# Attention heads in pairs: transposes, scores and value products of two heads in one run each, at fixed places; the gating of the attention branch behind the casts of gate a; the gate logits turned by full-size transposes; the upper halves first in the first query projection

## The chip, the cores and the metric

The kernel runs on one core of a Trainium2 chip. The metric is the time of one execution of the program on the device, in microseconds. The times of before are from three runs; the profile is of one more execution of its own.

## What is computed

An encoder trunk of two layers over 256 tokens of width 1024, all in float32. Each layer normalises its input, multiplies it by one wide matrix `w_in` (11 segments), and feeds two branches: a gated DeltaNet in both directions (with a short convolution over q, k and v) and differential attention. Gates close both branches, two projections and a sigmoid gate each merge them, and an output projection is added to the input. The attention branch is what the change touches:

```python
proj = h @ w_in[l]        # q_a, k_a, v_a, ab_a, z_a, q_b, k_b, v_b, z_b, gate_a, gate_b
# differential attention: 8 heads, each with two maps of width 64 and values of width 128
s = einsum('nbhqd,nbhkd->nbhqk', q_blk, k); p = softmax(s)
a = p[0] - lam * p[1]
o = einsum('bhqk,bhkd->bhqd', a, v)
o = rmsnorm(o, subln_w) * (1.0 - lambda_init);  y_b = o * silu(z_b)
merged = sigmoid(gate_a) * (y_a @ w_pa[l]) + sigmoid(gate_b) * (y_b @ w_pb[l])
```

`ab_a` holds the logits of DeltaNet's decay and write strength, 32 per token.

## The kernel before, in words

**Projections.** The 256 tokens are two tiles `m` of 128. To keep float32 accuracy, every weight is split into an upper half `hi` (rounded) and a lower half `lo = raw - hi`, and so is the activation; three products are added up: activation's upper part with hi (L324), with lo (L325), and its lower part with hi (L326). Weights come in four pairs of k-tiles (`kp`): one DMA of 512 KB into `raw`, a cast on ScalarE (L308, `hi_...`), a subtraction on VectorE (L310, `lo_...`). hi and lo have two buffers each, so the cast of a pair can begin when TensorE has used the pair two before. A name such as lo_zb012 is layer 0, half 1 of segment zb, pair 2; pp_zb010 is its sum for m = 0. `proj_tm` runs one such projection of 512 columns: 8 k-tiles by 2 m by 3 products, 48 matmuls.

**PSUM.** Eight banks: four in rotation for projections' sums (`banks2`, two at a time), two (`banks2_c`, `bank_c`) and two more (`bank`). The convolution's sums (pf_q, pf_k, pf_v), the scores of heads 0 and 1 and the sums of zb1 share the rotation of four; zb0's sums and the scores of the later heads use the pair `banks2_c`.

**Order.** Each engine works through its own queue in order. The tile scheduler sets the queues from the program text, priorities and explicit edges: `behind(x)` places an instruction after x. `mark` keeps instructions to be named so, and `place(n)` is the last matmul of k-tile n, counted on from zb0's first through zb0, zb1, za0, za1, gb0 and on, eight a projection.

**Attention.** The projections follow one another: qk (queries and keys, rotated by L602 to L605, turned by L608 and brought to `qkT` by ScalarE), conv v in between, zb0, zb1, za0, za1 (z of both branches), gb0, gb1 and ga0, ga1 (gates). Between their matmuls lie, head by head:
- `scores`: four 64-row matmuls (L1067; in the profile two records each, eight to a head), both maps side by side in the two halves of the array's rows, each map into a bank of its own (sc..1, sc..0); then VectorE's maxima (`mx`, L1075, one per map), ScalarE's exponentials with sums (L1077, four), and on VectorE a reciprocal (L1080), the factor `cc` (L1081) and two steps that subtract the second map (L1083, `es`);
- `turn`: four transposes of the map (L1094, `at`), copied by ScalarE (L1096, `aT`);
- `attend`: four products with v (L1105, `av`), copied by ScalarE into `ob` (L1109) and squared there with sums (L1111) for the norm.

Head h - 1 is turned shortly before the scores of head h, its product follows them. Heads 0 and 1 are scored within and right behind zb0.

VectorE has more to do there: the convolution of v (L679, `cvv`, four steps a channel tile, reading pf_v011 in PSUM until the last of them; L690), block transposes (L135), SiLU of z (L399, after ScalarE's tanh L398) and a forward substitution for DeltaNet's triangular solve (L868 and L869, `fstmp` and `X`), whose 31 steps are paced by the casts.

**Gating.** When the squares of all heads are there, `rb` is made (L1242 to L1245, with a power on POOL), and `gate_yb(i)` multiplies ob, rb and the gate (L1197) and turns the result in blocks (L249). Half 0 is placed behind casts of gb1, half 1 behind those of ga0.

**Logits.** `abp` (L630) has the 64 rows of both halves of the logits' weights, copied to `abT`; two matmuls with `id2` (L636, in the profile 64 rows by 32 columns) add the halves and turn them.

## Time and profile before

| | before |
|---|---|
| median of 3 runs | 742.87 us (742.01 to 742.99) |
| profiled execution | 742.73 us |
| its span, first to last instruction | 740.8 us |
| mean granted TensorE clock | 0.997 |
| busy: PE, DVE, ACT, POOL | 99%, 79%, 65%, 19% |
| moved from and to HBM | 182 GB/s over the span |

Times in rows of the profile are in us from the span's start. PE is TensorE's matmuls, PEld its weight loads, DVE VectorE, ACT ScalarE, POOL GpSimd. A row of a timeline gives start, duration (of a group: to the end of the last), engine, line, operation, output and inputs, shapes, and how many in a row; idle time and what ended it stand in brackets. A matmul's duration is longer than the distance to the next one, since matmuls are pipelined, so the distance between starts is what counts.

### The profile page before, as it was taken

To read this page: it belongs to the slowest core of one execution; us is meant where nothing else is said; L and a number is where in the kernel's file an instruction comes from. 1 tells how busy PE (TensorE), PEld (TensorE's weight loads), DVE (VectorE), ACT (ScalarE), POOL (GpSimd) and SP (SyncE) were. 2 spreads that over 40 slices of the span, in tenths; PEclk is the share of its full clock that TensorE was granted. 3 is DMA by queue.
4 is the path that set the end of the run, shared out by engine and by line. 5 is a ranking of instruction groups with operands and counts; after the bars stand their busy time and mean duration, and the time that the engine had idled before them with its cause. 6 is when DMAs were issued, how large, how long until landed. Compare 5 with 4: busy or idle time off the path is not lost.

```text
span 740.8 us, 13649 instructions
## 1 busy us (share of the span) xinstructions
PE 732.1 (99%) x5034; PEld 635.6 (86%) x5034; DVE 588.5 (79%) x1119; ACT 479.5 (65%) x1018; POOL 140.9 (19%) x223
## 2 busy tenths in 40 slices
PE   9999999999999999999999999999999999999996
PEld 6999889987888899888889899889788888998885
DVE  8696898999986885578667769999999769728782
ACT  6666875667876586645456578555787748665552
POOL 6004110112022433100000150202110514311000
PEclk9999999999999999999999999999999999999998
DMA  8755667776766473567674466767766736436641
GB/s 264 239 173 171 172 181 195 209 207 203 208 181 163 136 208 104 173 205 246 201 234 138 129 192 184 212 175 236 200 173 197 203 116 196 150 124 204 213 142 57
DMA packets 73732, 135.43 MB, mean 183 GB/s; under 512 B 12912, under 2 KB 13921, under 8 KB 73666
## 3 DMA queue, kind: packets, MB, share of 16 engines
q1 hardware_dynamic: 64750, 113.65, 51.6%
q0 software_dynamic: 7936, 19.35, 9.1%
q10 hardware_dynamic: 980, 1.58, 0.6%
q8 instruction: 39, 0.64, 0.4%
q14 instruction: 27, 0.22, 0.1%
HBM read 125.53 MB, written 9.01 MB: 182 GB/s over the span
## 4 chain that ended last, share of the span: by engine, by line
PE 96%; ACT 2%; issue 1%; DVE 1%; POOLq 0%; POOL 0%; DVEq 0%; ACTq 0%
PE pp_vb L369 4%; PE pp_qk L325 4%; PE pp_qk L326 3%; PE pp_qk L324 3%; PE sc L1067 2%; PE pp_o L369 2%; PE pp_za L325 2%; PE pf_k L385 2%; PE pf_v L385 2%; PE pf_v L389 2%; PE pp_ga L324 2%; PE pp_gb L324 2%; PE pp_zb L324 2%; PE pf_q L387 2%; PE pf_k L389 2%; PE pf_k L387 2%
## 5 line engine op out<-in xcount | busy, mean ns | idle before, releaser
L325 PE MATMUL pp_qk<-lo_qk,hT 128*128 128x512 f32 x128 | 50.5, 394 | 0.3
L326 PE MATMUL pp_qk<-hi_qk,hT 128*128 128x512 f32 x128 | 49.9, 390 | 0.0
L310 DVE TENSOR_TENSOR lo_qk<-raw_qk,hi_qk 128x1024 fp32r<-128x1024 f32 x32 | 39.1, 1221 | 12.0 <-ACT hi_qk L308 11.7
L324 PE MATMUL pp_qk<-hi_qk,hT 128*128 128x512 f32 x128 | 45.1, 393 | 0.0
L308 ACT CAST hi_qk<-raw_qk 128x1024 fp32r<-128x1024 f32 x28 | 29.4, 1049 | 23.4 <-PE pp_qk L326 12.7
L1077 ACT ACTIVATE es<-sc,mx 128x256 f32<-128x256 f32 x64 | 29.6, 473 | 19.5 <-DVE mx L1075 19.5
L385 PE MATMUL pf_q<-hT,hi_q 128*128 128x256 f32 x128 | 36.1, 285 | 0.0
L387 PE MATMUL pf_q<-hT,hi_q 128*128 128x256 f32 x128 | 35.9, 284 | 0.0
L385 PE MATMUL pf_k<-hT,hi_k 128*128 128x256 f32 x128 | 35.9, 286 | 0.0
L387 PE MATMUL pf_k<-hT,hi_k 128*128 128x256 f32 x128 | 35.9, 285 | 0.0
L385 PE MATMUL pf_v<-hT,hi_v 128*128 128x256 f32 x128 | 35.8, 285 | 0.0
L387 PE MATMUL pf_v<-hT,hi_v 128*128 128x256 f32 x128 | 35.8, 284 | 0.0
L389 PE MATMUL pf_q<-hT,lo_q 128*128 128x256 f32 x128 | 35.2, 288 | 0.0
L310 DVE TENSOR_TENSOR lo_pb<-raw_pb,hi_pb 128x1024 fp32r<-128x1024 f32 x16 | 19.6, 1225 | 18.9 <-ACT hi_pb L308 18.9
L389 PE MATMUL pf_v<-hT,lo_v 128*128 128x256 f32 x128 | 34.6, 288 | 0.0
L389 PE MATMUL pf_k<-hT,lo_k 128*128 128x256 f32 x128 | 34.3, 284 | 0.0
L308 ACT CAST hi_pa<-raw_pa 128x1024 fp32r<-128x1024 f32 x16 | 16.9, 1055 | 22.2 <-PE pp_pa L326 16.1
L679 DVE SCALAR_TENSOR_TENSOR cvq<-pf_q,cw,cvq 128x254 f32<-128x254 f32 (+1 forms) x64 | 30.0, 479 | 0.9 <-ACT cvq L675 0.4
L679 DVE SCALAR_TENSOR_TENSOR cvv<-pf_v,cw,cvv 128x254 f32<-128x254 f32 (+1 forms) x64 | 29.9, 479 | 0.1
L325 PEld LDWEIGHTS pp_qk<-lo_qk,hT 128*128 128x128 f32 x128 | 24.0, 188 | 6.6 <-DVE lo_qk L310 1.6
L679 DVE SCALAR_TENSOR_TENSOR cvk<-pf_k,cw,cvk 128x254 f32<-128x254 f32 (+1 forms) x64 | 28.5, 476 | 1.5 <-ACT cvk L675 0.9
L310 DVE TENSOR_TENSOR lo_pa<-raw_pa,hi_pa 128x1024 fp32r<-128x1024 f32 x16 | 19.6, 1224 | 11.2 <-ACT hi_pa L308 11.2
(416 smaller groups left out, 2535.1 us busy)
## 6 DMA issues: line engine op xcount, KB each, us to landing
raw_qk<-in_w_in_dram SPq DMA_DIRECT2D x32, 512.0 KB, 3.8
raw_k<-in_w_in_dram SPq DMA_DIRECT2D x16, 512.0 KB, 4.6
raw_q<-in_w_in_dram SPq DMA_DIRECT2D x16, 512.0 KB, 3.7
raw_v<-in_w_in_dram SPq DMA_DIRECT2D x16, 512.0 KB, 3.8
raw_zb<-in_w_in_dram SPq DMA_DIRECT2D x16, 512.0 KB, 4.0
raw_za<-in_w_in_dram SPq DMA_DIRECT2D x16, 512.0 KB, 3.8
raw_ga<-in_w_in_dram SPq DMA_DIRECT2D x16, 512.0 KB, 4.6
raw_pb<-in_w_pb_dram SPq DMA_DIRECT2D x16, 512.0 KB, 4.0
```

Source lines behind the costliest of these rows:

```text
L308: high = (V.tensor_copy if kp in turned else S.copy)(hi[:, :, :n], raw[:, :, :n]).ins
L310: mark[nm, kp] = high, V.tensor_tensor(lo[:, :, :n], raw[:, :, :n], hi[:, :, :n].bitcast(F32), ALU.subtract).ins
L324: T.matmul(o, act[kt // 4][:, 0, kt % 4, ts_], hi, start=kt == 0, stop=False)
L325: T.matmul(o, act[kt // 4][:, 0, kt % 4, ts_], lo, start=False, stop=False)
L326: mark["proj"] = T.matmul(o, act[kt // 4][:, 1, kt % 4, ts_], hi, start=False, stop=kt == KT - 1).ins
L369: mark["proj"] = T.matmul(o, act[kt // 4][:, pa, kt % 4, ts_], ws[kt][1 + pw], start=kt == 0 and n_ == 0, stop=kt == KT - 1 and n_ == 2).ins
L385: T.matmul(o, hi[:, cs], act[kt // 4][:, 0, kt % 4, :], start=first, stop=False, skip_group_check=True)
L387: T.matmul(o, hi[:, cs], act[kt // 4][:, 1, kt % 4, :], start=False, stop=False, skip_group_check=True)
L389: T.matmul(o, lo[:, cs], act[kt // 4][:, 0, kt % 4, :], start=False, stop=done, skip_group_check=True)
L679: V.scalar_tensor_tensor(ca[:, o0:o1], acc[:, b, o0 + sft : o1 + sft], cw[:, j, cb : cb + 1], ca[:, o0:o1], ALU.mult, ALU.add)
L1067: mm = T.matmul(sp[n][:, qt * SEQ : (qt + 1) * SEQ], qkT[h // 4][rows, 0, h % 4, qt * P : (qt + 1) * P], qkT[h // 4][rows, 1, h % 4, :], s ...
L1077: S.activation(es[:, n, qt, :], spv[:, qt, :], AF.Exp, bias=mx[:, n, qt : qt + 1], accum_out=s_all[:, h, n, qt : qt + 1])
```

## The change

It has four parts.

1. **Heads in pairs.** For p = 0 to 3 both heads of the pair before are turned (places 7, 12, 20, 27 of the count of k-tiles; heads 6 and 7 at 35), then both heads of pair p are scored, the second right behind the first, then the value products of the pair before go in one run into one bank and are copied at once. Head 2 and all even ones now take banks of the rotation of four; odd ones keep the pair.
2. **Gating behind casts.** `gate_yb` takes one tile (i, m) at a time: tile (0, 0) behind the cast of gb1's pair 2, the other three behind ga0's pairs 0, 1 and 2.
3. **Logits by full tiles.** `abT` gets 128 rows (64 of them zeros set by POOL) and is turned by two full transposes; the halves are added on VectorE.
4. **Upper first.** In the first query projection (qk00) all products with hi of the first two k-tiles come first, then those with lo.

```diff
@@ -109,8 +109,6 @@
     G.memset(ident, 1.0)
     G.affine_select(out=ident, in_=ident, compare_op=ALU.is_equal, fill=0.0,
                     base=0, pattern=[[1, P]], channel_multiplier=-1)
-    id2 = const.tile([64, 32], F32, name="id2")
-    V.tensor_tensor(id2, ident[0:64, 0:32], ident[0:64, 32:64], ALU.add)
     G.memset(tri, 1.0)
     for d, sg in ((0, 1), (1, -1)):
         G.affine_select(out=tri[:, d, :], in_=tri[:, d, :], compare_op=ALU.is_ge,
@@ -313,11 +311,20 @@
                 yield 2 * kp + k, hi[:, k, :n], lo[:, k, :n]
 
     def proj_tm(act, w, c0, n, evac, nm, places=(None,) * 4, spare=(), later=None, turned=(), between=None,
-                banks=None, held=None, first=(), raws={}):
+                banks=None, held=None, first=(), raws={}, upper=0):
 
         accs = (banks or banks2)(f"pp_{nm}")
-        for kt, hi, lo in weights(w, c0, n, nm, places, later=later, spare=spare, turned=turned, held=held,
-                                  first=first, raws=raws):
+        parts = weights(w, c0, n, nm, places, later=later, spare=spare, turned=turned, held=held,
+                        first=first, raws=raws)
+        ws = [next(parts) for _ in range(upper)]
+        for part in range(2 if ws else 0):
+            for kt, hi, lo in ws:
+                for m in range(NM):
+                    for pa in range(2 - part):
+                        mark["proj"] = mark["done", nm, kt] = T.matmul(
+                            accs[m][:, :n], act[kt // 4][:, pa, kt % 4, m * P : (m + 1) * P], lo if part else hi,
+                            start=not (kt or pa or part), stop=False).ins
+        for kt, hi, lo in parts:
             for m in range(NM):
                 ts_ = slice(m * P, (m + 1) * P)
                 o = accs[m][:, :n]
@@ -610,7 +617,7 @@
                     mark["qkT", m] = S.mul(qkT[i][:, s_, :, m * P : (m + 1) * P],
                                            pt.rearrange("p (b t) -> p b t", b=4), (DH ** -0.5, 1.0)[s_]).ins
                 proj_tm(hT, wl, (C_QB, C_KB)[s_] + 512 * i, 512, evac_qk, f"qk{l}{s_}{i}",
-                        turned=(0, 1) if (s_, i) == (0, 1) else ())
+                        turned=(0, 1) if (s_, i) == (0, 1) else (), upper=2 if (s_, i) == (0, 0) else 0)
 
 
 
@@ -629,13 +636,14 @@
             for part in range(2):
                 T.matmul(abp[0:64, :SEQ], wabr[:, kt, :], hT[kt // 4][:, part, kt % 4, :],
                          start=kt == 0 and part == 0, stop=kt == KT - 1 and part == 1)
-        abT = work.tile([64, SEQ], F32, tag="w2c", name=f"abT{l}", bufs=3)
-        mark["ab"] = S.copy(abT, abp[0:64, :SEQ]).ins
-        abq = bank_c(f"abq{l}")
+        abT = work.tile([P, SEQ], F32, tag="w2c", name=f"abT{l}", bufs=3)
+        G.memset(abT[64:P], 0.0)
+        mark["ab"] = S.copy(abT[0:64], abp[0:64, :SEQ]).ins
+        abq = bank_c(f"abq{l}")[:, :SEQ].rearrange("p (m c) -> p m c", m=NM)
         for m in range(NM):
-            T.matmul(abq[:, m * 32 : (m + 1) * 32], abT[:, m * P : (m + 1) * P], id2,
-                     start=True, stop=True)
-        V.tensor_copy(ab.rearrange("p m c -> p (m c)"), abq[:, :64])
+            T.transpose(abq[:, m, :], abT[:, m * P : (m + 1) * P], ident)
+        V.tensor_copy(ab, abq[:, :, 0:32])
+        V.tensor_tensor(ab, ab, abq[:, :, 32:64], ALU.add)
 
         a_ = small.tile([P, NM, 32], F32, tag="ga_", name=f"ga_{l}")
         V.tensor_scalar(a_[:, :, 0:16], ab[:, :, 0:16], -1.0, None, ALU.mult)
@@ -1059,7 +1067,7 @@
         def scores(h, after):
             es = work.tile([P, 2, NM, SEQ], F32, tag="w4a", name=f"es{l}{h}", bufs=2)
             mx = small.tile([P, 2, NM], F32, tag="mx", name=f"mx{l}{h}")
-            sp = (banks2 if h < 2 else banks2_c)(f"sc{l}{h}")
+            sp = (banks2_c if h > 1 and h % 2 else banks2)(f"sc{l}{h}")
             for qt in range(NM):
                 for n in (1, 0):
                     rows = slice(64 * n, 64 * n + 64)
@@ -1096,19 +1104,21 @@
                 S.copy(aT.rearrange("p k q -> p (k q)"), ap_)
             return aT
 
-        def attend(h, aT, after):
+        def attend(h0, maps, after):
             with tc.high_priority(offset=HP):
-                op_ = bank(f"av{l}{h}")
+                op_ = bank(f"av{l}{h0}").rearrange("p (q h e) -> p q h e", q=NM, h=2)
+                for h, aT in enumerate(maps, h0):
+                    for qt in range(NM):
+                        for kt in range(NM):
+                            with behind(after):
+                                T.matmul(op_[:, qt, h - h0], aT[:, kt, qt * P : (qt + 1) * P],
+                                         vb[h // 4][:, kt, h % 4 * P : h % 4 * P + P],
+                                         start=kt == 0, stop=kt == NM - 1)
+            oh = ob[h0 // 4][:, :, h0 % 4 * P : h0 % 4 * P + 2 * P].rearrange("p q (h e) -> p q h e", h=2)
+            S.copy(oh, op_)
+            for h in range(2):
                 for qt in range(NM):
-                    for kt in range(NM):
-                        with behind(after):
-                            T.matmul(op_[:, qt * P : (qt + 1) * P], aT[:, kt, qt * P : (qt + 1) * P],
-                                     vb[h // 4][:, kt, h % 4 * P : h % 4 * P + P],
-                                     start=kt == 0, stop=kt == NM - 1)
-            oh = ob[h // 4][:, :, h % 4 * P : h % 4 * P + P]
-            S.copy(oh, op_[:, :SEQ].rearrange("p (q e) -> p q e", q=NM))
-            for qt in range(NM):
-                S.activation(sqj[:, :P], oh[:, qt, :], AF.Square, accum_out=ssb[:, qt, h : h + 1])
+                    S.activation(sqj[:, :P], oh[:, qt, h], AF.Square, accum_out=ssb[:, qt, h0 + h : h0 + h + 1])
 
         zb = e4(f"zb{l}", "ex")
         za = [work.tile([P, NM, 512], F32, tag="w4c", name=f"za{l}_{i}", bufs=4) for i in range(2)]
@@ -1165,16 +1175,12 @@
         es = {}
         for p in range(4):
             z_part((zb, za)[p // 2], (C_ZB, C_ZA)[p // 2], ("zb", "za")[p // 2], p % 2)
-            for h in (2 * p, 2 * p + 1):
-                at = place((3, 7, 11, 15, 19, 23, 27, 31)[h])
-                aT = turn(h - 1, es[h - 1], at) if h > 2 else None
-                es[h] = scores(h, mark["at", h - 1] if h > 2 else place((3, 7, 12)[h]))
-                if h > 2:
-                    attend(h - 1, aT, mark["sc", h])
-                elif h == 1:
-                    attend(0, turn(0, es[0], place(7)), place(7))
-                elif h:
-                    attend(1, turn(1, es[1], place(11)), place(13))
+            two, at = (2 * p, 2 * p + 1), place((7, 12, 20, 27)[p])
+            maps = [turn(h, es[h], at) for h in range(two[0] - 2, two[0]) if p]
+            for h in two:
+                es[h] = scores(h, mark["sc", h - 1] if h % 2 else mark["at", h - 1] if p else at)
+            if p:
+                attend(two[0] - 2, maps, mark["sc", two[1]])
             substitute(names[p])
             if p == 0:
                 place_v(mark[f"zb{l}0", 1][0])
@@ -1227,9 +1233,9 @@
         wgb = big.tile([P, 2, 2, 512], F32R, tag="p8", name=f"wgb{l}", bufs=4)
         def last_head():
             weigh_q(0, 0, place(32))
-            aT = turn(7, es[7], place(34))
+            maps = [turn(h, es[h], place(35)) for h in (6, 7)]
             weigh_q(0, 1, place(36))
-            attend(7, aT, place(39))
+            attend(6, maps, place(38))
             weigh_q(1, 0, place(39))
 
         gtb = gate(C_GB, f"gb{l}", "ev",
@@ -1245,15 +1251,17 @@
         V.scalar_tensor_tensor(rb, rb, 0.5 * (1.0 - lam0), r0, ALU.mult, ALU.mult)
 
         ybT, yb_sent = pair(f"ybT{l}"), {}
-        def gate_yb(i):
-            at = [mark[f"ga{l}0", 1 + m][1] if i else mark[f"gb{l}1", 2 + m][1] for m in range(NM)]
+        def gate_yb(i, m, at):
             gated(lambda i, m: heads4(ob[i][:, m, :]), zb, rb, nw[:, 1:2], ybT, f"yb{l}",
-                  after={(i, m): at[m] for m in range(NM)}, halves_=(i,), sent=yb_sent)
-            for m in range(NM):
-                fetch(*yb_sent[i, m], None)
-
-        gate_yb(0)
-        gta = gate(C_GA, f"ga{l}", "eo", (lambda: gate_yb(1), None))
+                  (m,), {(i, m): at}, (i,), yb_sent)
+            fetch(*yb_sent[i, m], None)
+
+        def gate_others():
+            for kp, (i, m) in enumerate(((0, 1), (1, 0), (1, 1))):
+                gate_yb(i, m, mark[f"ga{l}0", kp][1])
+
+        gate_yb(0, 0, mark[f"gb{l}1", 2][1])
+        gta = gate(C_GA, f"ga{l}", "eo", (gate_others, None))
         for i, m in ((0, 0), (0, 1), (1, 0), (1, 1)):
             split_B(ybT[i], yb_sent[i, m][0], m, nw[:, 1:2], mark[f"ga{l}{i}", 2 + m])
         branch(ybT, w_pb[l], gtb, f"pb{l}")
```

Lines below the edit in `proj_tm` move: the products are L331 to L333 there, the casts L306 and L308, the scores L1075, mx L1083, the exponentials L1085.

**TensorE at zb0's end** (pp_zb00 is zb0's sum, pp_zb01 zb1's; sc00 and sc01 are the scores of heads 0 and 1). Before:

```order
L324 MATMUL pp_zb001_2026<-hi_zb003_2081,hT0_1_127 128x512
L325 MATMUL pp_zb001_2026<-lo_zb003_2082,hT0_1_127 128x512
L326 MATMUL pp_zb001_2026<-hi_zb003_2081,hT0_1_127 128x512
L1067 MATMUL sc011_2125<-qkT0_0_313 128x256
L1067 MATMUL sc010_2124<-qkT0_0_313 128x256
L1067 MATMUL sc011_2125<-qkT0_0_313 128x256
L1067 MATMUL sc010_2124<-qkT0_0_313 128x256
L324 MATMUL pp_zb010_2168<-hi_zb010_2170,hT0_0_126 128x512
L325 MATMUL pp_zb010_2168<-lo_zb010_2171,hT0_0_126 128x512
```

After:

```order
L332 MATMUL pp_zb001_2026<-lo_zb003_2082,hT0_1_125 128x512
L333 MATMUL pp_zb001_2026<-hi_zb003_2081,hT0_1_125 128x512
L1075 MATMUL sc001_2106<-qkT0_0_311 128x256
L1075 MATMUL sc000_2105<-qkT0_0_311 128x256
L1075 MATMUL sc001_2106<-qkT0_0_311 128x256
L1075 MATMUL sc000_2105<-qkT0_0_311 128x256
L1075 MATMUL sc011_2125<-qkT0_0_311 128x256
L1075 MATMUL sc010_2124<-qkT0_0_311 128x256
L1075 MATMUL sc011_2125<-qkT0_0_311 128x256
L1075 MATMUL sc010_2124<-qkT0_0_311 128x256
L331 MATMUL pp_zb010_2153<-hi_zb010_2155,hT0_0_124 128x512
L332 MATMUL pp_zb010_2153<-lo_zb010_2156,hT0_0_124 128x512
```

Head 0's four score matmuls, which stood amid zb0 between pairs 1 and 2, now stand at its end ahead of head 1's four; zb1's first matmul follows both.

**VectorE between lo_zb011 and lo_zb012** (mx00 and mx01 are the maxima of heads 0 and 1, thv the tanh of the convolution). Before:

```order
L310 TENSOR_TENSOR lo_zb011_2189<-raw_zb011_2190,hi_zb011_2188 128x1024
L1075 TENSOR_REDUCE mx01_2123<-sc011_2125 128x2
L399 SCALAR_TENSOR_TENSOR zb0_0_385<-zb0_0_385,pp_zb001_2026 128x512
L1075 TENSOR_REDUCE mx01_2123<-sc010_2124 128x2
L869 TENSOR_TENSOR X0_377<-X0_377,fstmp0_378 128x15x17
L690 SCALAR_TENSOR_TENSOR thv012_1890<-thv012_1890,cvv013_1893 128x256
L310 TENSOR_TENSOR lo_zb012_2207<-raw_zb012_2208,hi_zb012_2206 128x1024
```

After, the first twelve rows:

```order
L308 TENSOR_TENSOR lo_zb011_2174<-raw_zb011_2175,hi_zb011_2173 128x1024
L1083 TENSOR_REDUCE mx00_2104<-sc001_2106 128x2
L687 SCALAR_TENSOR_TENSOR cvv013_1893<-pf_v011_1738,cw0_298,cvv013_1893 128x254
L406 SCALAR_TENSOR_TENSOR zb0_0_385<-zb0_0_385,pp_zb001_2026 128x512
L1083 TENSOR_REDUCE mx00_2104<-sc000_2105 128x2
L877 TENSOR_TENSOR X0_377<-X0_377,fstmp0_378 128x15x17
L1088 RECIPROCAL cc00_2117<-s_all0_381 128x2
L698 SCALAR_TENSOR_TENSOR thv012_1890<-thv012_1890,cvv013_1893 128x256
L1083 TENSOR_REDUCE mx01_2123<-sc011_2125 128x2
L876 TENSOR_TENSOR fstmp0_378<-la0_375,X0_377 128x256
L1083 TENSOR_REDUCE mx01_2123<-sc010_2124 128x2
L133 STREAM_TRANSPOSE tb_v012_1901<-thv012_1890 128x512
```

Before, five steps stood between the two casts. After, the maxima of both heads stand there, and behind the rows shown come two factors cc, one more reciprocal, the four es steps of both heads and five steps of the substitution; only then comes lo_zb012, and lo_zb013 right behind it.

**VectorE from lo_ga000 to lo_ga002** (ktm are DeltaNet's keys, ob the attention's outputs). Before:

```order
L310 TENSOR_TENSOR lo_ga000_2896<-raw_ga000_2897,hi_ga000_2895 128x1024
L1004 TENSOR_TENSOR ktm0_360<-ktm0_360,kds0_372 128x512 x2
L310 TENSOR_TENSOR lo_ga001_2914<-raw_ga001_2915,hi_ga001_2913 128x1024
L1004 TENSOR_TENSOR ktm0_360<-ktm0_360,kds0_372 128x512 x2
L1197 SCALAR_TENSOR_TENSOR ob0_1_384<-ob0_1_384,rb0_2862,zb0_1_386 128x128 x4
L249 STREAM_TRANSPOSE zb0_1_386<-ob0_1_384 128x4x4x32
L310 TENSOR_TENSOR lo_ga002_2932<-raw_ga002_2933,hi_ga002_2931 128x1024
```

After:

```order
L308 TENSOR_TENSOR lo_ga000_2877<-raw_ga000_2878,hi_ga000_2876 128x1024
L1012 TENSOR_TENSOR ktm0_360<-ktm0_360,kds0_372 128x512 x2
L1203 SCALAR_TENSOR_TENSOR ob0_0_383<-ob0_0_383,rb0_2854,zb0_0_385 128x128 x4
L308 TENSOR_TENSOR lo_ga001_2895<-raw_ga001_2896,hi_ga001_2894 128x1024
L1012 TENSOR_TENSOR ktm0_360<-ktm0_360,kds0_372 128x512 x2
L1203 SCALAR_TENSOR_TENSOR ob0_1_384<-ob0_1_384,rb0_2854,zb0_1_386 128x128 x4
L247 STREAM_TRANSPOSE zb0_0_385<-ob0_0_383 128x4x4x32
L247 STREAM_TRANSPOSE zb0_1_386<-ob0_1_384 128x4x4x32
L308 TENSOR_TENSOR lo_ga002_2913<-raw_ga002_2914,hi_ga002_2912 128x1024
```

Four more products with rb and one more block transpose now stand ahead of lo_ga002; they stood ahead of lo_ga000 before. Ahead of these rows lo_gb013 and one step of B have moved behind rb.

## Prediction

> **What bounds the kernel now.** I read the page first: busy time, clock and chain.
>
> ```profile
> PE 732.1 (99%) x5034; PEld 635.6 (86%) x5034; DVE 588.5 (79%) x1119; ACT 479.5 (65%) x1018; POOL 140.9 (19%) x223
> ...
> PEclk9999999999999999999999999999999999999998
> ...
> PE 96%; ACT 2%; issue 1%; DVE 1%; POOLq 0%; POOL 0%; DVEq 0%; ACTq 0%
> ```
>
> TensorE is busy throughout at full clock, and 96% of the chain that ended last is its own work. A matmul taken away there is time gained; any new wait of TensorE is time lost. So the second reading is TensorE's waits: only one is long, and it lies before the first real matmul.
>
> ```profile
> PE idle L410 <- DVE ones L407: 1.1, 1, 1.1
> ```
>
> The third is who could make it wait. The change moves work in the stretch where head 0 and head 1 start, so I asked for the busy time of that window. The columns are the length, then busy time (and count) of PE, PEld, DVE, ACT and POOL, the clock, the DMA share and GB/s.
>
> ```profile
> 155.00:185.00 30.00, 30.00 (x151) 23.53 (x149) 29.97 (x68) 22.56 (x57) 4.12 (x8) 1.00 0.68 198
> ```
>
> This is the row that decides. The page's 79% for VectorE is an average; in these 30 us it has 0.03 us free. Whatever holds VectorE up here goes through its casts (lo_zb) to TensorE.
>
> **What the change saves on TensorE.** First the scores. The timeline of the second run of head scores, with two looks inside it:
>
> ```profile
> 170.84 0.40 PE L325 MATMUL pp_zb<-lo_zb,hT 128*128 128x512 f32 x1
> 171.07 0.40 PE L326 MATMUL pp_zb<-hi_zb,hT 128*128 128x512 f32 x1
> 171.40 1.14 PE L1067 MATMUL sc<-qkT 64*128 64x256 f32 x8
> 172.46 0.50 PE L324 MATMUL pp_zb<-hi_zb,hT 128*128 128x512 f32 x1
> 172.80 0.40 PE L325 MATMUL pp_zb<-lo_zb,hT 128*128 128x512 f32 x1
> ...
> 171.72 0.81 PE L1067 MATMUL sc<-qkT 64*128 64x256 f32 x6
> 171.94 0.60 PE L1067 MATMUL sc<-qkT 64*128 64x256 f32 x4
> ```
>
> Matmuls of 512 columns follow each other every 0.23 us (170.84, 171.07), and pairs of score records, one in each half of the rows, every 0.22 (171.72, 171.94). From 171.07 to 172.80 pass 1.73 us; two 512s (0.46) and four pairs (0.86) explain 1.32. Going into the run of 64-row matmuls and out again costs the other 0.41. Two heads in one run leave 8 runs of 16: four times 0.41, so 1.64 us a layer.
>
> The Trainium skill's page "TensorEngine Tiling (Array Packing)", under Key Properties, says that changing the tiling mode drains TensorE, without a figure. The drain of 128 cycles at 2.4 GHz that "TensorE: Matmul & The Clock Gate" gives (step-by-step, 4) would be an estimated 0.05 us each way, and with that the eight runs would bring 0.8 us in all instead of 3.3; the measured 0.41 a run decides.
>
> The small projection abq and the first products of queries are the other two savings:
>
> ```profile
> 27.17 0.28 PE L389 MATMUL pf_k<-hT,lo_k 128*128 128x256 f32 x1
> 27.38 0.63 PE L636 MATMUL abq<-id,abT 64*128 64x32 f32 x4
> 27.94 0.39 PE L385 MATMUL pf_k<-hT,hi_k 128*128 128x256 f32 x1
> 28.16 0.28 PE L387 MATMUL pf_k<-hT,hi_k 128*128 128x256 f32 x1
> ...
> 164.84 0.66 PE L608 MATMUL qkt<-ident,stg 128*128 128x128 f32 x4
> ...
> 80.20 0.61 PE L324 MATMUL pp_qk<-hi_qk,hT 128*128 128x512 f32 x2
> 80.96 0.50 PE L325 MATMUL pp_qk<-lo_qk,hT 128*128 128x512 f32 x1
> ...
> 79.68 1.22 DVE L310 TENSOR_TENSOR lo_qk<-raw_qk,hi_qk 128x1024 fp32r<-128x1024 f32 x1
> ```
>
> 27.17 to 28.16 is 0.99, of which two 256s would be 0.24: abq costs 0.75. Four full-width transposes end 0.66 after their start, so I take 0.11 each and 0.22 for the new two: 0.53 saved. At 80.96 a lo matmul starts 0.30 later than 80.20 + 2 x 0.23 and with 0.1 of restart behind it: it waited for the cast that ended at 80.90. That is the third pair of k-tiles of qk00; with upper first the first pair's hi buffer is free four matmuls sooner, and the order puts that lo ahead of the convolution steps. I take the 0.41 as gone. The memset on POOL, one more add of 64 columns and half as many copies of ob are hidden by engines that are idle there (POOL 19%); uncovered, each is below 1 us.
>
> Saved: 1.64 + 0.53 + 0.41 = 2.6 us a layer, 5.2 in all.
>
> **What it adds: waits at four places in each layer.** Their prices come from these rows of VectorE's and ScalarE's timelines. An operation holds VectorE from its start to the next one's start, about 0.08 less than its duration.
>
> ```profile
> 172.07 0.68 DVE L399 SCALAR_TENSOR_TENSOR zb<-zb,pp_zb 128x512 f32<-128x512 f32 x1
> 172.67 0.48 DVE L679 SCALAR_TENSOR_TENSOR cvv<-pf_v,cw,cvv 128x254 f32<-128x254 f32 x1
> 173.06 0.42 DVE L868 TENSOR_TENSOR fstmp<-la,X 128x255 f32<-128x255 f32 x1
> 173.39 0.88 DVE L1083 SCALAR_TENSOR_TENSOR es<-es,cc 128x256 f32<-128x256 f32 x2
> 174.18 1.22 DVE L310 TENSOR_TENSOR lo_zb<-raw_zb,hi_zb 128x1024 fp32r<-128x1024 f32 x1
> 175.32 0.69 DVE L1075 TENSOR_REDUCE mx<-sc 128x2 f32<-128x512 f32 x1
> 175.92 0.68 DVE L399 SCALAR_TENSOR_TENSOR zb<-zb,pp_zb 128x512 f32<-128x512 f32 x1
> ...
> 179.32 0.70 DVE L135 STREAM_TRANSPOSE tb_v<-thv 128x512 f32<-128x512 f32 x1
> ...
> 180.24 0.22 DVE L1081 SCALAR_TENSOR_TENSOR cc<-s_all,neglam,cc 128x2 f32<-128x2 f32 x1
> ```
>
> ```profile
> 171.01 0.61 ACT L398 ACTIVATE zb<-pp_zb 128x512 f32<-128x512 f32 x1
> 171.55 1.04 ACT L308 CAST hi_zb<-raw_zb 128x1024 fp32r<-128x1024 f32 x1
> ...
> L1077 ACT ACTIVATE es<-sc,mx 128x256 f32<-128x256 f32 x64 | 29.6, 473 | 19.5 <-DVE mx L1075 19.5
> ...
> 181.53 0.31 ACT L1111 ACTIVATE sqj<-ob 128x128 f32<-128x128 f32 x1
> ...
> 181.97 0.31 ACT L1111 ACTIVATE sqj<-ob 128x128 f32<-128x128 f32 x1
> ```
>
> *First, the start of zb1.* Before, head 0 was scored amid zb0, so its bank had been read long before zb1 took it for its sums. Now its scores stand at zb0's end, head 1's right behind, and then zb1, whose first matmul needs the bank of sc001: it waits for two exponentials, they for mx, and mx stands on VectorE behind lo_zb011. Head 1's scores in turn need banks that conv v holds until its last step, just behind that mx. Count from the start of zb0's last matmul (171.07 before). The tanh ends at 0.55; then L399, a conv step, a step of the substitution (0.60 + 0.39 + 0.33) and lo_zb011 from 1.94; mx from 3.08 to 3.77; the conv step to 4.15. Head 1's four pairs end at 5.05 (0.86), zb1 starts near 5.15, and the exponentials (to 4.7) are done by then. Without waits the run of two heads would have let zb1 start at 0.33 + 1.06 + 0.86 = 2.25. The wait is 2.9. If lo_zb011 goes as soon as its hi cast is there (1.52), mx starts at 2.66 and the exponentials end at 4.3: 2.0. I take 2.8, nearer the full queue, since VectorE has no gap here.
>
> *Second, lo_zb012 in zb1's middle.* The order puts both heads' softmax between lo_zb011 and lo_zb012; before, one head's maxima stood there. From mx at 3.08: mx, conv, L399, mx end at 5.36, and the reciprocal behind waits for two exponentials more, to 6.4. Then to the second reciprocal 3.0 (thv and X at 0.33, two mx 1.2, fstmp 0.33, the transpose 0.62, cc 0.13, the rest small), and 3.1 more (two pairs of es at 0.79, four substitution steps at 0.33, cc): lo_zb012 from 12.5, done at 13.7. TensorE wants it 26 matmuls (24 of pairs 0 and 1, two of pair 2) behind zb1's start, at 5.15 + 26 x 0.23 = 11.1. The wait is 2.6; if VectorE needn't idle for the exponentials, 1.9. I take 2.4.
>
> *Third, the second pair of za0 and of za1.* ScalarE now has eight exponentials in a row, then the first pair's hi cast, a copy of two heads' ob, four squares and a tanh ahead of the second hi: 0.95 + 0.5 (the copy, by the tanh of as many elements) + 4 x 0.44 + 0.5 = 3.7 from the first cast to the second, against 2.7 for TensorE's twelve matmuls. Some of this is covered by the lead of the first cast; I take 0.4 each, 0 to 0.8.
>
> *Fourth, lo_ga002.* Here the gating moves behind the casts:
>
> ```profile
> 247.97 3.17 ACT L951 ACTIVATE U__96<-zt 32x256 f32<-32x256 f32 x8 [4.14 <-PE zt L943]
> ...
> 252.79 1.23 DVE L310 TENSOR_TENSOR lo_ga<-raw_ga,hi_ga 128x1024 fp32r<-128x1024 f32 x1
> ...
> 257.47 1.14 DVE L1197 SCALAR_TENSOR_TENSOR ob<-ob,rb,zb 128x128 f32<-128x128 f32 x4
> 258.64 1.14 DVE L249 STREAM_TRANSPOSE zb<-ob 128x512 f32<-128x512 f32 x1
> 259.61 1.23 DVE L310 TENSOR_TENSOR lo_ga<-raw_ga,hi_ga 128x1024 fp32r<-128x1024 f32 x1
> ...
> 261.08 0.40 PE L325 MATMUL pp_ga<-lo_ga,hT 128*128 128x512 f32 x1
> ```
>
> lo_ga002 ends at 260.84 and is wanted at 261.08: 0.24 to spare. Four gating products and a transpose (1.1 + 1.0) now stand between lo_ga000 and it. lo_ga000 may start 0.6 sooner, as the work ahead needs only U (251.14) and two transposes. So 2.1 - 0.6 - 0.24 = 1.2; 0 if rb comes soon enough for all the gating to go ahead, 1.8 if nothing is gained.
>
> Sum per layer: 2.8 + 2.4 + 0.8 + 1.2 = 7.2 lost, 2.6 saved: 4.6 slower, 9.2 for two layers. On the profiled run (742.73; its span is 740.8) that is 751.9, on the median (742.87) **752**. The bounds: 2.0 + 1.9 alone lost gives 1.3 a layer, 745.5; 2.9 + 2.6 + 1.6 + 1.8 = 8.9 gives 6.3, 755.5; if VectorE, full already at 155, cannot take up the 0.9 a layer saved ahead of zb0, 757.
>
> **The rivals.** *The casts keep up* (0.15): the waits fall away, because VectorE reaches lo_zb011 earlier, having no softmax of head 0 ahead of it. Then the saving stands: 742.87 - 5.2 = 737.7. For it: TensorE waits for no cast of this stretch in the list of waits today. Against it: 29.97 of 30. It decides at 1.3 us: if zb1's start and lo_zb012 together wait under 1.3 a layer and the later places not at all, half of the saving is left. Around no change (within 0.2%, 1.5 us, about what a measurement of this kernel can tell) the chance is 0.05.
>
> *Only zb1 waits* (0.2): the places in za and ga have cover that I don't see; 2 x (5.2 - 2.6) = 5.2 slower, 748.
>
> *The clock falls* (0.05): after a wait the granted clock drops and the matmuls behind run slower. At half clock for as long as each of zb1's waits, half of 5.2 is lost again a layer: 5.2 in all, 757. Against: the longest wait in the trace, 1.1 us, left PEclk at 9. The page "TensorE: Matmul & The Clock Gate" of the Trainium skill (What's actually happening) has the clock go to half after an idle window of about 3.4 us; by that rule waits of 2.9 and 2.6, parted by 26 matmuls, stay just under it, and no row here shows one.
>
> **How the numbers follow.** The forecast's own case (all four places) has 0.55, only zb1 0.2, the clock 0.05: slower 0.8. Range 744.5 to 757, from the lower bound of the two waits at zb1 (745.5, less 1 us for the size of the savings) to the upper sum; it leaves out the gain and the cases around no change, 0.2.
>
> **What would show it.** In the profile after: TensorE's waits list the exponentials or conv v at the first scores of head 1 and zb1's first matmul, and DVE lo_zb under zb1, 2 to 3 us each, once a layer; DVE lo_ga about 1. The score runs come eight at 16 records, each costing 0.41 less than two. A list of waits without lo_zb, or TensorE's time before zb0 not 0.9 a layer shorter, shows me wrong; so does a wait at sc11 or zb1 under 1 us.

## The result, and the profile after

The changed kernel takes **756.16 us** (median of four runs, 755.36 to 757.52) against 742.82 before (four runs, 742.01 to 742.99): a ratio of 1.0178 (95% interval 1.0165 to 1.0192). It is slower, as forecast, by 13.3 us where 9 were forecast. The profiled execution took 755.36 us, its span is 753.4 and its mean granted clock 0.995.

Busy time, clock and chain on the page after:

```profile
PE 734.4 (97%) x5030; PEld 637.5 (85%) x5030; DVE 591.1 (78%) x1120; ACT 479.3 (64%) x1010; POOL 141.0 (19%) x225
...
PEclk9999999999999999999999999999899999999999
...
PE 71%; DVE 14%; ACT 8%; issue 4%; DMA 1%; SPq 0%; DVEq 0%; POOLq 0%; POOL 0%; ACTq 0%
```

TensorE's own share of the chain that ended last fell from 96% to 71%; VectorE has 14% of it now and ScalarE 8%. One slice of the clock, the twenty-ninth, is no longer 9. TensorE's waits say where (total, times, longest):

```profile
PE sc L1075 <- DVE cvv L687: 4.4, 2, 2.2
PE pp_zb L332 <- DVE lo_zb L308: 2.0, 2, 1.5
PE pp_ga L332 <- DVE lo_ga L308: 1.4, 2, 0.7
PE pp_qk L332 <- DVE lo_qk L308: 1.4, 2, 0.7
PE pp_za L332 <- DVE lo_za L308: 1.3, 4, 0.4
PE idle L417 <- DVE ones L414: 1.1, 1, 1.1
PE pp_gb L332 <- DVE lo_gb L308: 0.8, 2, 0.4
```

Every row but the idle one is new, and each comes once or twice a layer. The decisive window of before, now:

```profile
155.00:185.00 30.00, 26.34 (x129) 20.46 (x130) 28.37 (x64) 20.50 (x47) 5.47 (x10) 1.00 0.61 179
```

TensorE was busy for all of these 30 us; 3.7 of them are idle now. Its timeline at zb0's end and in zb1's middle:

```profile
169.77 1.56 PE L1075 MATMUL sc<-qkT 64*128 64x256 f32 x10
173.54 1.10 PE L1075 MATMUL sc<-qkT 64*128 64x256 f32 x6 [2.21 <-DVE cvv L687]
174.56 0.50 PE L331 MATMUL pp_zb<-hi_zb,hT 128*128 128x512 f32 x1
...
182.32 0.50 PE L332 MATMUL pp_zb<-lo_zb,hT 128*128 128x512 f32 x1 [1.45 <-DVE lo_zb L308]
...
184.32 2.00 PE L1075 MATMUL sc<-qkT 64*128 64x256 f32 x16
186.25 0.50 PE L331 MATMUL pp_zb<-hi_zb,hT 128*128 128x512 f32 x1
```

Both heads' scores form one run, but it breaks inside head 1: ten records, 2.21 idle, six records. The run at 184.32 shows the saving undisturbed. VectorE between the two casts:

```profile
171.17 1.23 DVE L308 TENSOR_TENSOR lo_zb<-raw_zb,hi_zb 128x1024 fp32r<-128x1024 f32 x1
172.31 0.69 DVE L1083 TENSOR_REDUCE mx<-sc 128x2 f32<-128x512 f32 x1
172.91 0.48 DVE L687 SCALAR_TENSOR_TENSOR cvv<-pf_v,cw,cvv 128x254 f32<-128x254 f32 x1
...
176.16 0.69 DVE L1083 TENSOR_REDUCE mx<-sc 128x2 f32<-128x512 f32 x1
...
177.89 0.86 DVE L1091 SCALAR_TENSOR_TENSOR es<-es,cc 128x256 f32<-128x256 f32 x2
...
179.47 0.87 DVE L1091 SCALAR_TENSOR_TENSOR es<-es,cc 128x256 f32<-128x256 f32 x2
...
181.05 2.35 DVE L308 TENSOR_TENSOR lo_zb<-raw_zb,hi_zb 128x1024 fp32r<-128x1024 f32 x2
```

The last convolution step ends at 173.39, and head 1's scores go on at 173.54: that step freed their bank. The next cast stands behind the softmax of two heads, from 172.31 to 181.05.

The logits' projection after, at the place where abq cost 0.75:

```profile
26.70 0.28 PE L396 MATMUL pf_k<-hT,lo_k 128*128 128x256 f32 x1
26.82 0.38 PE L644 MATMUL abq<-ident,abT 128*128 128x128 f32 x2
26.95 0.36 PE L392 MATMUL pf_k<-hT,hi_k 128*128 128x256 f32 x1
27.15 0.28 PE L394 MATMUL pf_k<-hT,hi_k 128*128 128x256 f32 x1
```

From 26.70 to 27.15 pass 0.45, of which two 256s are 0.24: 0.21 is left, so 0.54 came out of it.

The end of qk00, on VectorE, and the matmul that waits for it:

```profile
79.48 2.55 DVE L687 SCALAR_TENSOR_TENSOR cvq<-pf_q,cw,cvq 128x254 f32<-128x254 f32 x6
81.95 1.21 DVE L308 TENSOR_TENSOR lo_qk<-raw_qk,hi_qk 128x1024 fp32r<-128x1024 f32 x1
```

```profile
83.22 0.50 PE L332 MATMUL pp_qk<-lo_qk,hT 128*128 128x512 f32 x1 [0.68 <-DVE lo_qk L308]
```

The cast of the fourth pair stands behind six convolution steps, and TensorE waits for it, at a pair where it did not before.

In layer 1 the first wait has a second cost. The columns of these windows end in the granted clock, the DMA share and GB/s; behind them two matmuls of the same stretch:

```profile
540.00:543.00 3.00, 1.51 (x6) 1.20 (x6) 3.00 (x8) 1.76 (x7) 0.00 (x0) 0.65 0.92 265
543.00:546.00 3.00, 3.00 (x8) 2.06 (x7) 3.00 (x8) 1.72 (x9) 0.56 (x1) 0.50 0.18 71
546.00:549.00 3.00, 3.00 (x11) 2.36 (x11) 2.97 (x10) 0.91 (x4) 1.08 (x3) 0.71 0.22 90
```

```profile
545.33 0.63 PE L332 MATMUL pp_zb<-lo_zb,hT 128*128 128x512 f32 x1
545.76 0.63 PE L333 MATMUL pp_zb<-hi_zb,hT 128*128 128x512 f32 x1
```

The three means 0.65, 0.50 and 0.71 make 6.8 us at half clock, from 540.9 to 547.7. Behind zb1's start (543.46) matmuls follow each other every 0.43 us, not 0.23, for 4 us. In layer 0 behind the same wait the clock stayed at 1.00.

### The profile page after: what moved, and what is told of

Its sections match the earlier page's. It is cut to its first block, busy times and chain, and to the rows that moved or that the text cites. A ratio compares the mean times of both kernels' runs of the same rounds, so it can differ in the third digit from the quotient of the medians.

```text
span 753.4 us, 13629 instructions
## 1 busy us (share of the span) xinstructions
PE 734.4 (97%) x5030; PEld 637.5 (85%) x5030; DVE 591.1 (78%) x1120; ACT 479.3 (64%) x1010; POOL 141.0 (19%) x225
## 4 chain that ended last, share of the span: by engine, by line
PE 71%; DVE 14%; ACT 8%; issue 4%; DMA 1%; SPq 0%; DVEq 0%; POOLq 0%; POOL 0%; ACTq 0%
PE pp_vb L376 4%; ACT es L1085 3%; PE pp_qk L332 3%; PE pp_qk L333 2%; PE pp_qk L331 2%; PE pp_o L376 2%; PE pf_v L392 2%; DVE lo_za L308 2%; PE pf_k L392 2%; PE pf_v L396 2%; PE pf_k L396 2%; PE pf_q L394 2%; PE pf_k L394 2%; PE pf_q L392 2%; PE pf_v L394 2%
## 5 line engine op out<-in xcount | busy, mean ns | idle before, releaser
L308 DVE TENSOR_TENSOR lo_qk<-raw_qk,hi_qk 128x1024 fp32r<-128x1024 f32 x32 | 39.1, 1221 | 15.3 <-ACT hi_qk L306 15.0
L332 PE MATMUL pp_qk<-lo_qk,hT 128*128 128x512 f32 x120 | 47.1, 393 | 1.4 <-DVE lo_qk L308 1.4
L333 PE MATMUL pp_qk<-hi_qk,hT 128*128 128x512 f32 x120 | 46.8, 390 | 0.0
L306 ACT CAST hi_qk<-raw_qk 128x1024 fp32r<-128x1024 f32 x28 | 29.4, 1049 | 22.8 <-PE pp_qk L333 12.1
L331 PE MATMUL pp_qk<-hi_qk,hT 128*128 128x512 f32 x120 | 42.3, 393 | 0.0
L1085 ACT ACTIVATE es<-sc,mx 128x256 f32<-128x256 f32 x64 | 29.5, 474 | 12.2 <-DVE mx L1083 12.2
L308 DVE TENSOR_TENSOR lo_pb<-raw_pb,hi_pb 128x1024 fp32r<-128x1024 f32 x16 | 19.6, 1224 | 20.7 <-ACT hi_pb L306 20.7
L306 ACT CAST hi_pa<-raw_pa 128x1024 fp32r<-128x1024 f32 x16 | 16.9, 1055 | 22.2 <-PE pp_pa L333 16.0
L308 DVE TENSOR_TENSOR lo_pa<-raw_pa,hi_pa 128x1024 fp32r<-128x1024 f32 x16 | 19.6, 1223 | 11.1 <-ACT hi_pa L306 11.1
```

The source lines that it names most:

```text
L306: high = (V.tensor_copy if kp in turned else S.copy)(hi[:, :, :n], raw[:, :, :n]).ins
L308: mark[nm, kp] = high, V.tensor_tensor(lo[:, :, :n], raw[:, :, :n], hi[:, :, :n].bitcast(F32), ALU.subtract).ins
L331: T.matmul(o, act[kt // 4][:, 0, kt % 4, ts_], hi, start=kt == 0, stop=False)
L332: T.matmul(o, act[kt // 4][:, 0, kt % 4, ts_], lo, start=False, stop=False)
L333: mark["proj"] = T.matmul(o, act[kt // 4][:, 1, kt % 4, ts_], hi, start=False, stop=kt == KT - 1).ins
L1085: S.activation(es[:, n, qt, :], spv[:, qt, :], AF.Exp, bias=mx[:, n, qt : qt + 1], accum_out=s_all[:, h, n, qt : qt + 1])
```

## The experiments

**The parts alone.** The first question is which of the four parts costs what. Three kernels are the kernel before with one part; the fourth has the pairs alone.

```diff
...
-                        turned=(0, 1) if (s_, i) == (0, 1) else ())
+                        turned=(0, 1) if (s_, i) == (0, 1) else (), upper=2 if (s_, i) == (0, 0) else 0)
```

> The kernel before with the upper halves first in the first query projection alone. Theory of the waits: the third pair's wait (0.4 us) goes, but lo_qk of the fourth pair comes 0.8 late behind six convolution steps, since VectorE's order changes: 0.5 us a layer slower, 742.8 + 1.0 = about 743.9. Rival (the prediction's step): the wait of 0.4 goes and nothing takes its place, 742.0.

Measured: 743.69 us against 742.46, ratio 1.0018 (1.0009 to 1.0027), slower by 1.2. Its waits:

```profile
PE pp_qk L334 <- DVE lo_qk L310: 1.4, 2, 0.7
```

The row is that of the whole change. Upper first loses by itself.

```diff
...
-        gate_yb(0)
-        gta = gate(C_GA, f"ga{l}", "eo", (lambda: gate_yb(1), None))
+        gate_yb(0, 0, mark[f"gb{l}1", 2][1])
+        gta = gate(C_GA, f"ga{l}", "eo", (gate_others, None))
```

> The kernel before with the gating behind casts alone. Theory of the waits: only lo_ga002 is late, 0.9 us a layer as in the trace of after; 742.8 + 1.8 = about 744.6. Rival, that the wait at lo_ga002 comes from the pairs (their later squares and rb) and not from the place of the gating: no wait there, 742.8 or a little less.

Measured: 744.25 us against 742.46, 1.0020 (1.0011 to 1.0030), slower by 1.8, with this wait:

```profile
PE pp_ga L325 <- DVE lo_ga L310: 1.4, 2, 0.7
```

So the gating loses by itself too, at the cast of ga's third pair.

```diff
...
-            T.matmul(abq[:, m * 32 : (m + 1) * 32], abT[:, m * P : (m + 1) * P], id2,
-                     start=True, stop=True)
-        V.tensor_copy(ab.rearrange("p m c -> p (m c)"), abq[:, :64])
+            T.transpose(abq[:, m, :], abT[:, m * P : (m + 1) * P], ident)
+        V.tensor_copy(ab, abq[:, :, 0:32])
+        V.tensor_tensor(ab, ab, abq[:, :, 32:64], ALU.add)
```

> The kernel before with the logits by full tiles alone. Both theories: 0.5 us a layer less on TensorE at the logits' two runs, 742.8 - 1.0 = about 741.8, unless VectorE's order elsewhere changes with it.

Measured: 741.34 us against 742.46, 0.9985 (0.9975 to 0.9995): faster by 1.1, twice 0.54. It is the one part that gains, and by itself it is faster than either kernel.

```diff
...
-            for h in (2 * p, 2 * p + 1):
-                at = place((3, 7, 11, 15, 19, 23, 27, 31)[h])
...
+            two, at = (2 * p, 2 * p + 1), place((7, 12, 20, 27)[p])
+            maps = [turn(h, es[h], at) for h in range(two[0] - 2, two[0]) if p]
...
```

> The kernel before with the heads in pairs alone. If the parts add up: 756.2 less upper first (+1.2 measured) and the gating (+1.8), and without the logits' gain (-1.1): about 754.3, with TensorE's waits at head 1's scores, lo_zb, lo_za and lo_gb and none at lo_qk and lo_ga. Rival, that the waits of the parts overlap (a later TensorE gives lo_ga time): 755.5 or more.

Measured: 752.69 us against 742.59, 1.0140 (1.0121 to 1.0159): slower by 10.1. Its waits are those of the whole change at sc, lo_zb, lo_za and lo_gb, and none at lo_qk or lo_ga. The time is 1.6 under the 754.3 that was expected: the single parts add up to 10.1 + 1.8 + 1.2 - 1.1 = 12.0 of 13.3. The rest is of the size of the clock's share. In this profile the clock is at half for 3.4 us in layer 1, not for 6.8, and from zb0's first matmul to za0's first pass 35.2 us there, not 36.5. So three quarters of the loss are the pairs.

**Which wait of the pairs.** The changed kernel with heads 0 and 1 scored apart again, at their places of before:

```diff
-                es[h] = scores(h, mark["sc", h - 1] if h % 2 else mark["at", h - 1] if p else at)
+                es[h] = scores(h, (mark["sc", h - 1] if h % 2 else mark["at", h - 1]) if p else place((3, 7)[h]))
```

> The kernel after, with the first two heads scored apart as before (head 0 behind k-tile 3 of zb0, head 1 behind its last); everything else of the change stays. Theory of the waits: zb1 no longer waits at head 1's scores and at lo_zb012, which cost 2.9 and 1.7 us a layer in the trace of after, nor does the clock fall behind them in layer 1 (about 1.9 us); one run of scores more a layer costs 0.4. 756.2 - 9.2 - 1.9 + 0.8 = about 746. Rival, that pairs themselves are what is slow (long runs of 64-row matmuls, wide copies on ScalarE), wherever they stand: three of four pairs are left, so no more than a quarter of the 13 us comes back, about 753.

Measured: 753.57 us against 742.46, 1.0148 (1.0133 to 1.0163). The wait ahead of zb1 is gone and that for lo_zb is down to 0.8 in all, as the theory has it, but the time is the rival's. The rival's mechanism is not what the trace shows: a new row heads TensorE's waits, and ScalarE's timeline in layers 0 and 1 shows why:

```profile
PE pp_za L331 <- ACT hi_za L306: 3.9, 2, 2.9
```

```profile
189.28 1.28 ACT L734 ACTIVATE vtm<-tb_v,nrm 128x128 f32<-128x128 f32 x4 [2.12 <-DMA tb_v<-bnc_v]
...
557.01 1.28 ACT L734 ACTIVATE vtm<-tb_v,nrm 128x128 f32<-128x128 f32 x4 [3.97 <-DMA tb_v<-bnc_v]
```

With TensorE earlier than in the changed kernel, ScalarE comes to the scaled copies of v before their DMA has landed and stands there; eight exponentials and the next hi cast stand behind. In layer 1 that wait of 2.9 us brings the clock down again:

```profile
564.00:567.00 3.00, 2.48 (x9) 1.60 (x8) 2.78 (x5) 1.72 (x5) 0.00 (x0) 0.74 0.27 39
```

Whether that copy's place is all of it, the next run tells: the same kernel with the copies one cast later.

```diff
...
             elif p == 2:
-                place_v(mark[f"za{l}0", 1][0])
+                place_v(mark[f"za{l}0", 2][0])
```

> The changed kernel with heads 0 and 1 scored apart again, and with the last four scaled copies of v (vtm) behind the third cast of za0 in place of the second. In the run without that second edit ScalarE stood 2.1 us (layer 0) and 4.0 us (layer 1) at those copies for a DMA, the eight exponentials of heads 2 and 3 behind it, and TensorE waited for hi_za 3.9 us in all (753.57). Theory (that DMA wait at the head of ScalarE's queue makes the hi_za wait): the wait for hi_za falls under 0.8 in all and the time is 749.5 to 750.5. Rival (the eight exponentials themselves, 3.6 us between two casts that TensorE uses up in 2.8, are enough): hi_za still waits 2 us or more in all, 751.5 to 753.5.

Measured: 747.20 us against 742.86, 1.0060 (1.0044 to 1.0075). No hi_za in TensorE's waits; the longest row is now

```profile
PE pp_za L332 <- DVE lo_za L308: 1.8, 4, 0.6
```

The theory holds and the rival falls, and the gain is larger than expected: in the profiles 1.2 us in layer 0 and 3.0 in layer 1 of wait, and 1.5 more behind it in layer 1, where the matmuls no longer run at half clock. Against the changed kernel 9.0 us are back, by the two edits together. The copies of v were not moved alone; in the changed kernel ScalarE's waits list none for their DMA.

**Bank or queue at zb1.** The break inside head 1's scores can come of the bank that conv v holds, or of TensorE waiting for VectorE's queue in any case. Here head 1's scores take two banks of the transposes, and zb1 is held behind them; with that zb1's sums come to other banks of the rotation.

```diff
...
-            sp = (banks2_c if h > 1 and h % 2 else banks2)(f"sc{l}{h}")
+            sp = ([bank(f"sc{l}{h}{i}") for i in range(2)] if h == 1 else
+                  (banks2_c if h % 2 else banks2)(f"sc{l}{h}"))
...
```

> The kernel after with head 1's scores in two banks of their own (those of the transposes, free at that time), and zb1 held behind them as it stands now. Theory of the queue: head 1 no longer waits for conv v, but zb1's first matmul still waits for the exponentials of sc001, which stand behind lo_zb011 and mx: the wait shrinks from 2.9 to about 2.1, and lo_zb012 (earlier in VectorE's order) ends about 1 us sooner a layer; about 754.2, or 752.5 if the clock no longer falls. Rival, that the shared bank is the whole cause: no wait ahead of zb1, 2.9 a layer back, about 750 or less.

Measured: 754.63 us against 742.59, 1.0156 (1.0140 to 1.0172). TensorE at the same places:

```profile
170.30 0.40 PE L334 MATMUL pp_zb<-hi_zb,hT 128*128 128x512 f32 x1
170.63 2.00 PE L1077 MATMUL sc<-qkT 64*128 64x256 f32 x16
172.56 0.50 PE L332 MATMUL pp_zb<-hi_zb,hT 128*128 128x512 f32 x1
...
179.31 0.73 PE L332 MATMUL pp_zb<-hi_zb,hT 128*128 128x512 f32 x2 [1.02 <-ACT hi_zb L306]
181.25 0.79 PE L333 MATMUL pp_zb<-lo_zb,hT 128*128 128x512 f32 x1 [1.21 <-DVE lo_zb L308]
```

```profile
180.00:183.00 3.00, 1.79 (x5) 1.38 (x5) 3.00 (x6) 1.37 (x5) 1.10 (x3) 0.65 0.46 107
```

Neither theory had it whole. The bank is the cause of the first wait: without it the run is unbroken. The queue is the bound behind it: TensorE comes to the third pair of zb1 earlier, and hi_zb012 stands behind eight exponentials, lo_zb012 behind the es steps; two waits of 1.0 and 1.2 a layer, and a clock that here is at half for 3.4 us in each layer, take most of the gain back. Removed ahead of a full queue, the wait moved to the queue's next customer.

**The squares.** The changed kernel with the squares of heads 0 to 3 placed behind the second hi cast of the next projection:

```diff
...
+            if p > 1:
+                mark["squares"](mark[names[p], 1][0])
```

> The kernel after with the squares of heads 0 to 3 placed behind the second hi cast of the next projection instead of ahead of it on ScalarE. Theory: lo_za's two waits (1.2 us a layer with the restarts) come from ScalarE's queue, where four squares and a copy stand ahead of hi_za; 1.76 us of squares gone from there, they vanish: 756.2 - 2.4 = about 753.8. Rival, that VectorE's queue or the DMA of the weights makes lo_za late: no change.

Measured: 753.86 us against 742.59, 1.0159 (1.0135 to 1.0184), 2.3 below the changed kernel by the medians, and in the waits

```profile
PE pp_za L332 <- DVE lo_za L308: 0.4, 2, 0.2
```

in place of 1.3 at four places. So ScalarE's row of small work between two hi casts is a cause of the waits in za. That the theory's time came out is luck all the same. From za0's first matmul to gb0's first the run is only 0.4 us a layer shorter: za1's wait is gone and za0's is smaller, but za0's third pair now starts 0.4 late. Another 1.3 lie in layer 1 between the first matmuls of zb0 and za0 (35.2 us, not 36.5), ahead of the squares: there the clock is at half for 3.4 us in this profile, not for 6.8.

**The clock.** The changed kernel with ten 128 by 128 matmuls of the identity ahead of head 1's scores; their result is never read.

```diff
+                if h == 1:
+                    warm = bank(f"warm{l}")
+                    for _ in range(10):
...
+                            mm = T.matmul(warm[:, :P], ident, ident, start=True, stop=True)
...
```

> The kernel after with ten idle matmuls (128x128, result never read, about 2.2 us) between the scores of heads 0 and 1, where TensorE waits 2.4 us in any case. Theory: in layer 1 the granted clock falls because TensorE stands still there; with the idle matmuls it stays at 1.00 through both waits and about 1.9 us come back, 754.3, with less spread between runs. Rival, that the clock falls for another reason (power, the work behind): the clock falls all the same, 756.2 or more.

Measured: 754.12 us against 742.59, 1.0152 (1.0136 to 1.0167), 2.0 below the changed kernel although work was added. The window that had 0.65:

```profile
540.00:543.00 3.00, 3.00 (x27) 2.54 (x23) 3.00 (x6) 1.38 (x3) 0.89 (x2) 1.00 0.81 251
```

The mean clock of each of the four executions is 0.999 here, and 0.990 to 0.995 in those of the changed kernel. So it is TensorE's standing still that takes the clock down.

**All mended.** The kernel with heads 0 and 1 apart and the copies of v one cast later, with the squares moved, the gating as before and no upper first:

```diff
-                        turned=(0, 1) if (s_, i) == (0, 1) else (), upper=2 if (s_, i) == (0, 0) else 0)
+                        turned=(0, 1) if (s_, i) == (0, 1) else ())
...
+                mark["squares"](mark[names[p], 1][0])
...
-        gate_yb(0, 0, mark[f"gb{l}1", 2][1])
-        gta = gate(C_GA, f"ga{l}", "eo", (gate_others, None))
+        gate_yb(0)
+        gta = gate(C_GA, f"ga{l}", "eo", (lambda: gate_yb(1), None))
```

> The run beside it (heads 0 and 1 apart, vtm behind the third cast of za0) with three parts of the change undone or moved as well: the gating as before, no upper first in qk00, the squares of heads 0 to 3 behind the second cast of the next projection. By the single runs these three bring 1.8, 1.2 and 2.3 us (the last at most, since vtm's place differs). If the parts add up: 5 below the run beside it, so 744.5 to 746 by the theory and 747 to 748.5 by its rival. If below 742, pairing heads 2 to 7 and the logits pay once their waits are mended; if above 747.5, the parts do not add up and the pairs of heads 2 to 7 have a wait of their own.

Measured: 742.48 us against 742.86, 0.9995 (0.9985 to 1.0004): 4.7 below the run beside it, near the 5 of additive parts, and no different from the kernel before. The sum agrees better than its terms: by the starts of TensorE's matmuls, both layers together, 1.1 comes back in qk (1.2 expected), 1.2 in za0 and za1 (2.3 at most) and 2.8 from gb0 to ga1 (1.8). What it still waits for:

```profile
PE pp_za L332 <- DVE lo_za L308: 1.2, 2, 0.6
...
PE pp_zb L332 <- DVE lo_zb L308: 0.8, 2, 0.4
...
PE pp_gb L332 <- DVE lo_gb L308: 0.7, 2, 0.4
```

Three of four pairs save 3 x 0.41 a layer, 2.5 in all, and these waits cost 2.7. Pairing heads 2 to 7 pays nothing here: the logits' gain of 1.1 is still in this kernel, and only 0.4 of it is left. The logits alone, 741.34, stay the best version.

## Why the prediction was right, and where its steps were off

Term by term, for a layer, in us; measured are the starts of TensorE's matmuls in layer 0 after against before. A wait has its restart with it: the matmul that ends it is followed by the next one 0.1 us later than usual (0.34 in place of 0.23).

| step | predicted | measured |
|---|---|---|
| four score runs of eight gone | -1.64 | -1.64 |
| abq | -0.53 | -0.54 |
| qk00, upper first | -0.41 | +0.54 |
| start of zb1 | 2.8 | 2.9 |
| lo_zb012 | 2.4 | 1.8 |
| second pairs of za0 and za1 | 0.8 | 1.2 |
| lo_gb000 | not listed | 0.7 |
| lo_ga002 | 1.2 | 0.9 |
| sum | 4.6 | 5.9 |

The layer as a whole grew by 5.6, from its first projection to the first matmul of pb, the projection behind ga1; the 0.3 between is not placed. In layer 1 the stretch from zb0 to ga1 grew by 7.9, in layer 0 by 5.6. Most of that difference lies between the first matmuls of zb0 and za0, where it is 1.9 (8.16 against 6.22): the clock. It is the half clock's cost less 0.9, by which lo_zb012 waits less there, since TensorE comes to it later. The first products started 0.4 earlier, and the stretch behind ga1 of layer 1 was 0.4 shorter: 5.6 + 7.9 - 0.8 = 12.7, where the profiled runs differ by 12.6.

- **The savings** were right to a few hundredths. From the matmul ahead of a run to the one behind pass 1.27 us in every run of eight behind transposes before, 2.13 in every run of sixteen after: 2 x 1.27 - 2.13 = 0.41. The drain of 128 cycles in the Trainium skill's page "TensorE: Matmul & The Clock Gate" (the estimate of 0.05 each way in the prediction) is far too little for it.
- **The start of zb1** was right in its place and size, and the prediction named both candidates, the exponentials and the bank of conv v. It was the bank: 2.21 idle ahead of head 1's scores, none ahead of zb1's own first matmul.
- **lo_zb012** was mis-sized by 0.6, and its wait was 1.45 in layer 0 and 0.53 in layer 1, not the 2 to 3 that were to show in the list. The prediction let VectorE idle for the exponentials before the reciprocals and took 2.4 over its lower case of 1.9. VectorE filled that time with the convolution and the substitution; the cast began 11.6 us behind zb0's last matmul (169.44), not 12.5.
- **za and gb.** The step was the right one, ScalarE's row between two hi casts, and the squares' experiment confirms it for za, though only a third of the loss came back by it. But the same row stands ahead of gb0's first cast: eight exponentials, a copy and two squares ahead of hi_gb000 in ScalarE's timeline. The prediction counted two places, not three; this third one is read from the timeline, and no run moved it alone.
- **qk00 was the step that failed**: "upper first puts that lo ahead of the convolution steps" holds for the third pair, whose wait is gone (0.43). The fourth pair's lo then stands behind six convolution steps, 0.97 lost. The prediction followed the change to the first cast that it helped and not to the next one in the same queue. So its own sign of being wrong came: TensorE's time before zb0 was to be 0.9 a layer shorter, and is 149.4 us from the first projection to zb0 in both profiles of layer 0.
- **The clock** was a rival of 0.05 by its mechanism, 757 us by its price. It came, in layer 1 alone, and at 1.9 us. It did not come in place of the forecast but on top of it: with the terms above, 1.0 a layer over the forecast, it makes most of the 4 us that the time lies over 752, near the range's end. That it was not further off is partly luck: the terms that were too small (qk00, za, gb) come to 2.1 a layer, those that were too large (lo_zb012, lo_ga002) to 0.9.
- **The rivals that were faster or equal** fall with the list of waits; "only zb1 waits" (748) falls with the waits at za, gb and ga.

## What to carry to other kernels

Fewer changes of the array's shape are worth their 0.41 us each only where the engines behind have slack; read VectorE's and ScalarE's free time in the very window, and follow the moved order to every cast behind it, not only to the first. Joining two heads on TensorE also joins their softmax into one block on the other two engines, and a cast that stood between now stands behind. Price the parts of a bundle one by one: here one part of four gained. And when an expected time comes out, look in the trace whether it came from the expected stretch: with the squares most of it did not.

## What the hardware did that was not expected

Waits well under 3 us took the granted clock to half. It fell behind 2.19 us of idle in layer 1 (0.50 in the window behind), behind 1.02 and 1.21 with two matmuls between, and behind 2.87, but not behind 2.21 in layer 0. The stretches at half clock before the kernel's end last 6.8 us in the changed kernel and 3.4 in the four other profiles that have one (pairs alone, heads apart, squares, head 1 in banks of its own). In the last of these it falls in both layers, 368.6 us apart, which is 108 times 3.413.

The Trainium skill's page "TensorE: Matmul & The Clock Gate" (What's actually happening) gives two states, full and half, and a free-running window of about 3.4 us that judges activity. The two states agree (0.43 against 0.23 between matmuls), and so do these lengths and the distance. That the window must be idle throughout does not fit: no gap here was 3.4 us long.

Steps of 3.413 us, counted back and forth from the fall at 540.89, show why the same wait counted in one layer only. The columns are as in the windows above; the first figure behind the length is TensorE's busy time:

```profile
168.84:172.25 3.41, 2.49 (x15) 1.53 (x13) 3.41 (x7) 2.14 (x3) 2.17 (x4) 1.00 0.81 250
172.25:175.66 3.41, 2.12 (x11) 1.61 (x12) 3.41 (x9) 2.34 (x9) 0.00 (x0) 1.00 0.84 251
537.48:540.89 3.41, 1.81 (x12) 1.06 (x10) 3.41 (x8) 1.80 (x3) 1.73 (x4) 1.00 0.82 231
540.89:544.30 3.41, 2.81 (x8) 1.94 (x9) 3.41 (x10) 2.41 (x10) 0.00 (x0) 0.50 0.71 198
```

In layer 0 the wait was shared between two steps, with 0.9 and 1.3 us idle; in layer 1 1.6 us fell into one, and the clock fell at its end. Where a wait lies against these steps nobody planned; the mean clocks of the changed kernel's four executions, 0.990 to 0.995, differ too. Counted in this way in all the profiles that show a fall, no step at full clock with up to 1.48 us idle was followed by half clock, and every one with 1.98 or more was; in between, 1.60 and 1.86 were and 1.76 and 1.87, both at the kernel's end, were not. So idle time alone is not the whole measure, and no run varied it on purpose. Ten short matmuls within the gap kept the clock.
